# Product order, staging of the last row tiles and VectorE order in a Strassen-Winograd matmul with logsumexp

## The chip, the cores and the metric

The kernel runs on one core of one Trainium2 chip. The metric is the device time of one execution in microseconds. Each kernel is run several times, together with the kernel before on the same chip. Most executions of a kernel agree within 0.3%; some of the kernel before are up to 2.5% slower and are left out as slow runs. Ratios in this document are the mean time of one kernel's fast runs over that of the other's, so they are not quite the ratio of the medians that are quoted. A profiled execution's span is about 2 us shorter than its time. All spans and positions are of profiled runs.

Engines in the profile: PE is the matmul side of TensorE, PEld its weight loads, DVE is VectorE, ACT is ScalarE, POOL is GpSimd, SP is SyncE.

## The reference

```python
m, k, n = 1024, 4096, 4096
a = np.random.randn(m, k).astype(np.float32)
b = np.random.randn(k, n).astype(np.float32)
x = np.matmul(a, b)
return special.logsumexp(x, axis=-1).astype(np.float32)
```

## The kernel before

Both operands become fp16. The columns of B are taken in eight blocks of 512. The rows of A are eight tiles of 128, taken in pairs; a pair, a block and all of k make a *quad*. A quad is computed by the Strassen-Winograd scheme: seven products M1 to M7 of 16 matmuls (128x128 weights, 256 columns) in place of eight. Two PSUM rows, r0 and r1, hold the four quarters of the result: c11 and c12 are the halves of r0, c21 and c22 those of r1. ScalarE copies some products out of PSUM, VectorE adds them, then come a row maximum on VectorE and an exponential on ScalarE. VectorE also makes the sums of B that some products need (T1, T4, T6 in new tiles, T3 and T7 in place) and the sums of A; the rows of one pair in `aT` are a *slab* of A (one text below also calls a quarter of a B block so). The last quad of a step (step 6 apart), in which most sums of the next block are made, is called a *tail*. In the code, KP is 16 (all of k, 256 rows at a time), GI is 4 (a quarter of k), H is 256 columns, MT is 8 row tiles and MP 4 row pairs.

The work has this shape in time. Block 0 is multiplied plainly while A and B arrive (until about 63 us). Step 0 is block 1 for three row pairs at once (the *joint* quads). Steps 1 to 6 are blocks 2 to 7, four quads each. Two more quads finish blocks 0 and 1 for the last row pair. That pair is not transposed on TensorE as the first three are: GpSimd's DMA queue casts the two row tiles to fp16 in DRAM (the *staging* copies), and SyncE's DMA queue transposes them from there into `aT`. Step 1's fourth quad needs them first, after VectorE has made five sums of that slab.

```python
a_m = a.rearrange("(p mt) k -> mt p k", mt=MT)       # row tile, 128 rows, k
...
        def load(self, lo, hi):                       # a quarter of a B block
            nc.gpsimd.dma_start(out=self.raw[lo // GI][...], in_=b_rows[:, lo:hi, :, ts(self.nb, FD)])
...
        if more:
            ...
                nxt = plan[step + 1][0]().load_all()
        if step == 0:
            a16 = dram_pool.tile([2, P, K], f16, name="a16")
            for m in range(2):
                nc.gpsimd.dma_start(out=a16[m], in_=a_m[MT - 2 + m])      # staging
            for m in range(2):
                nc.sync.dma_start_transpose(
                    aT[:, :, :, MP - 1, m, :].rearrange("p i t c -> p (i t) c"), a16[m])
...
            s = fix_pool.tile([P, 4, H], f32, name=f"s_{step}_{q}", tag="s")   # one buffer
            x, e = s[:, 1::2], s[:, 0:2]              # x[:, 0] is the place of e[:, 1]
            ...                                       # M1, M5 -> r0; copy e; M2, M6 -> r1
            nc.scalar.copy(out=s[:, 2], in_=c21)
            flush()                                   # exponentials of the quad before
            add(s[:, 2], s[:, 2], e[:, 1])
            sub(s[:, 0], s[:, 2], e[:, 0])
            ...
            m3(c12)
            nc.scalar.copy(out=x[:, 0], in_=c12)
            m7(c11)
            m4(c21)
            nc.scalar.copy(out=x[:, 1], in_=c21)
            sub(x, x, s[:, 0::2])
            add(c22, c22, x[:, 0])
            add(c11, c11, x[:, 1])
            ...
            for h in range(2):
                lse_max(rows[h], 2 * q + h, nb)
                pending.append(...)                   # lse_exp, run by the next flush
            if step == 1 and q == 1:
                a_sums_early(slice(0, KP), MP - 1)    # sums of the last slab of A
                a_sums_late(slice(0, KP), MP - 1)
```

## Time and profile before

| | before |
|---|---|
| time, median of 20 runs | 455.34 us (453.89 to 462.8) |
| span of the profiled run | 453.5 us |
| PE busy | 93% |
| one product of 16 matmuls, start to start | 1.747 us |
| a full quad, start to start | 12.85 us (7 x 1.747 = 12.23) |
| nine last products of the three joint quads | 83.95 to 113.0 us |

These are lines of the page of the kernel before. Each digit is the busy share of one of 40 slices of 11.3 us in tenths; `PEclk` is the granted TensorE clock, `DMA` the busy share of the 16 DMA engines, `GB/s` what they moved.

```profile
span 453.5 us, 8512 instructions
PE 422.7 (93%) x3647; PEld 350.5 (77%) x3647; DVE 258.7 (57%) x566; ACT 109.6 (24%) x278; POOL 73.1 (16%) x114
...
PEclk9999999986999999999999999999999999999998
DMA  8999999999994069300990059400990049599000
```

TensorE is nearly always busy; DMA is full for the first 12 slices, then works about 40% of the time (the mean of the other 28 digits). PE dips in the slices around 90 to 113 us, and there the clock falls too. The waits of PE say why (columns: who waited, for whom; us in total, times, longest):

```profile
PE acc_2_0_761 L366 <- ACT s_2_1130 L493: 4.5, 1, 4.5
PE acc_1_0_759 L366 <- ACT s_1_1061 L493: 3.3, 1, 3.3
...
PE acc_2_0_1471 L366 <- ACT s_2_1473 L493: 1.1, 1, 1.1
...
PE acc_0_0_2295 L366 <- ACT s_0_2297 L493: 0.5, 1, 0.5
```

L493 is ScalarE's copy of M3's result, and the waiter is M7. The last line is one of 25 alike, one for nearly every quad. The timeline shows one of these quads (start, duration, engine, line, instruction, how many):

```profile
211.71 0.60 PE L366 MATMUL acc_3_0_2139<-b_3_1205,aT 128*128 128x256 f16 x4
...
212.35 0.37 ACT L493 COPY s_3_2141<-acc_3_0_2139 128x256 f32<-128x256 f32 x1
...
212.77 0.60 PE L366 MATMUL acc_3_0_2139<-b_0_1202,aT 128*128 128x256 f16 x4 [0.46 <-ACT s_3_2141 L493]
```

M3's last four matmuls start at 211.71 us and M7 would follow 0.44 us later, at 212.15. It starts at 212.77: 0.62 us are lost per quad. The two products write the halves of one row, and the copy reads that row.

The last row tiles cost nothing visible here. Their two staging copies are down 34 us after they are issued, most of it spent in the queue, and the transposes run beside the loads of the next B block. These are the lines of the DMA issues (out, in, queue, count, size of one, us from issue to landing):

```profile
a_752<-in_a_dram POOLq DMA_DIRECT2D x2, 1024.0 KB, 34.0
...
aT<-a_752 SPq DMA_TRANSPOSE x2, 20.7
```

### The profile page before, as it was taken

The numbers are of one execution on the slowest core, as the hardware profiler recorded it, in microseconds if no ns is written. First come the engines' busy times: TensorE is split into PE (matmuls) and PEld (weight loads), VectorE is DVE, ScalarE is ACT, GpSimd is POOL, SyncE is SP. The second block draws the span as 40 slices with busy tenths as digits, with TensorE's granted clock in tenths as the row PEclk, the third lists the DMA queues.
The fourth block names the chain that finished last, engine by engine and source line by source line (L and its number), as shares of the span: only waits on it lengthen the run. The fifth ranks groups of instructions, "written<-read, shape, count | busy, mean of one in ns | idle before, by whom it ended". The sixth has DMA issues, their size and how long they took to land.

```text
span 453.5 us, 8512 instructions
## 1 busy us (share of the span) xinstructions
PE 422.7 (93%) x3647; PEld 350.5 (77%) x3647; DVE 258.7 (57%) x566; ACT 109.6 (24%) x278; POOL 73.1 (16%) x114
## 2 busy tenths in 40 slices
PE   7999999976999999999999999999999999999994
PEld 2554568854888888888888888888888888888883
DVE  1557687555737595218832585127922485175995
ACT  1222240122222122222221222222211222222214
POOL 7776751003000030001100030000200030110000
PEclk9999999986999999999999999999999999999998
DMA  8999999999994069300990059400990049599000
GB/s 120 202 203 203 194 202 206 207 214 219 197 180 71 1 103 207 63 1 2 198 172 1 1 90 207 76 2 1 187 185 1 1 77 207 89 192 180 1 2 0
DMA packets 57493, 52.97 MB, mean 117 GB/s; under 512 B 10096, under 2 KB 57200, under 8 KB 57200
## 3 DMA queue, kind: packets, MB, share of 16 engines
q0 software_dynamic: 49056, 50.34, 67.4%
q1 hardware_dynamic: 8400, 2.10, 3.1%
q8 instruction: 28, 0.46, 0.4%
q14 instruction: 9, 0.07, 0.0%
HBM read 100.66 MB, written 2.10 MB: 227 GB/s over the span
## 4 chain that ended last, share of the span: by engine, by line
PE 79%; DVE 9%; ACT 6%; DMA 4%; issue 1%; POOL 1%; DVEq 0%; ACTq 0%; POOLq 0%
DMA tb<-in_a_dram 4%; PE acc_0_0_757 L366 2%; PE acc_3_0_4311 L366 2%; PE acc_1_0_4043 L366 2%; PE acc_2_0_3631 L366 2%; PE acc_1_0_2423 L366 2%; PE acc_3_0_2139 L366 2%; PE acc_2_0_2011 L366 2%; PE acc_1_0_2963 L366 2%; PE acc_3_0_2679 L366 2%; PE acc_2_0_2551 L366 2%; PE acc_1_0_1883 L366 2%; PE acc_3_0_1599 L366 2%; PE acc_2_0_4175 L366 2%; PE acc_3_0_3759 L366 2%; PE acc_1_0_3503 L366 2%
## 5 line engine op out<-in xcount | busy, mean ns | idle before, releaser
L366 PEld LDWEIGHTS <-aT 128*128 128x128 f16 x1856 | 183.8, 99 | 48.2 <-issue 25.3
L366 PEld LDWEIGHTS <-s_71 128*128 128x128 f16 x464 | 45.4, 98 | 5.5
L366 PEld LDWEIGHTS <-s_73 128*128 128x128 f16 x464 | 45.4, 98 | 5.3
L366 PEld LDWEIGHTS <-s_72 128*128 128x128 f16 x464 | 45.4, 98 | 5.3
L192 POOL DMA_DIRECT2D tb<-in_a_dram x48 | 26.0, 544 | 7.5 <-PE tps_98 L203 1.5
L203 PEld LDWEIGHTS <-tb 128*128 128x128 f16 x192 | 13.9, 99 | 16.7 <-DMA tb<-in_a_dram 10.3
L221 PEld LDWEIGHTS <-aT 128*128 128x128 f16 x192 | 16.8, 98 | 11.9 <-ACT aT L216 0.3
L216 ACT COPY aT<-tps_98 128x512 f16<-128x512 f16 x24 | 14.0, 585 | 44.3 <-PE tps_98 L203 44.3
L214 DVE COPY aT<-tps_97 128x512 f16<-128x512 f16 x24 | 10.2, 425 | 25.5 <-PE tps_97 L203 25.4
L84 DVE TENSOR_TENSOR aT<-aT 128x256 f16<-128x256 f16 (+2 forms) x54 | 16.0, 350 | 0.0
L203 PE MATMUL tps_97<-ident,tb 128*128 128x128 f16 x96 | 9.6, 224 | 1.7 <-DMA tb<-in_a_dram 1.7
L203 PE MATMUL tps_98<-ident,tb 128*128 128x128 f16 x96 | 9.3, 219 | 1.0 <-DMA tb<-in_a_dram 1.0
L81 DVE TENSOR_TENSOR s_71<-aT 128x256 f16<-128x256 f16 (+1 forms) x25 | 8.1, 323 | 2.1 <-ACT aT L216 2.1
L138 POOL DMA_DIRECT2D b_0_1747<-in_b_dram x1 | 0.9, 881 | 50.8 <-PE acc_3_0_1599 L366 50.8
L138 POOL DMA_DIRECT2D b_0_2827<-in_b_dram x1 | 0.9, 890 | 47.9 <-PE acc_3_0_2679 L366 47.9
L138 POOL DMA_DIRECT2D b_0_2287<-in_b_dram x1 | 0.9, 878 | 47.9 <-PE acc_3_0_2139 L366 47.9
L138 POOL DMA_DIRECT2D b_0_3907<-in_b_dram x1 | 0.9, 881 | 47.9 <-PE acc_3_0_3759 L366 47.9
L138 POOL DMA_DIRECT2D b_0_3367<-in_b_dram x1 | 0.9, 878 | 47.9 <-PE acc_3_0_3219 L366 47.9
L81 DVE TENSOR_TENSOR s_73<-aT 128x256 f16<-128x256 f16 (+1 forms) x25 | 8.1, 324 | 0.0
L81 DVE TENSOR_TENSOR s_72<-aT 128x256 f16<-128x256 f16 (+1 forms) x25 | 8.1, 323 | 0.0
L282 PE MATMUL acc_1_96<-s_73 128*128 128x512 f16 x15 | 6.5, 570 | 1.2 <-DVE s_73 L285 1.2
L138 POOL DMA_DIRECT2D aT<-in_b_dram x4 | 3.5, 890 | 24.2 <-PE acc_1_1_4044 L366 24.2
(1045 smaller groups left out, 899.0 us busy)
## 6 DMA issues: line engine op xcount, KB each, us to landing
tb<-in_a_dram POOLq DMA_DIRECT2D x48, 128.0 KB, 5.9
aT<-in_b_dram POOLq DMA_DIRECT2D x4, 1024.0 KB, 14.7
a_752<-in_a_dram POOLq DMA_DIRECT2D x2, 1024.0 KB, 34.0
b_0_83<-in_b_dram POOLq DMA_DIRECT2D x4, 256.0 KB, 6.0
b_1_84<-in_b_dram POOLq DMA_DIRECT2D x4, 256.0 KB, 6.2
b_2_85<-in_b_dram POOLq DMA_DIRECT2D x4, 256.0 KB, 6.4
b_3_86<-in_b_dram POOLq DMA_DIRECT2D x4, 256.0 KB, 6.2
b_0_87<-in_b_dram POOLq DMA_DIRECT2D x2, 512.0 KB, 8.6
```

The costliest lines, as they stand in the source:

```text
L81: nc.vector.tensor_tensor(out=o, in0=x, in1=y, op=ALU.add)
L84: nc.vector.tensor_tensor(out=o, in0=x, in1=y, op=ALU.subtract)
L138: nc.gpsimd.dma_start(out=self.raw[lo // GI][:, lo % GI : lo % GI + hi - lo], in_=b_rows[:, lo:hi, :, ts(self.nb, FD)],)
L192: nc.gpsimd.dma_start(out=slot, in_=a_m[m, :, k0 * P : (k0 + kn) * P])
L203: nc.tensor.matmul(pst[:, ts(j, P)], src[:, ts(j, P)], ident, is_transpose=True, start=(j == 0), stop=(j == kn - 1),)
L214: nc.vector.tensor_copy(out=dst, in_=v)
L216: nc.scalar.copy(out=dst, in_=v)
L221: nc.tensor.matmul(pt, aT[:, i, kp, m // 2, m % 2, :], blk0.raw[i // GI][:, i % GI, kp, :], start=(done[m] == 0), stop=(done[m] == KT - 1),)
L282: nc.tensor.matmul(acc[2][1], zeros[:, 0:P], zeros[:, 0:FD], start=True, stop=True)
L366: nc.tensor.matmul(c, lhs(i), rhs(i), start=(start and i == 0), stop=(i == KP - 1), skip_group_check=True,)
```

## The change

The change has three parts. The product order in each quad becomes M3, M4, M7, so that M4, which writes the other row, runs while ScalarE copies M3's result. The last two row tiles come in k halves: a staging copy for both tiles and one half of k, then two half transposes, and so on; the slab's sums are split to match, and GpSimd holds back the last two of the four B loads of step 2 (block 3) until the first half is transposed, by an instruction that reads one of its rows (the *gate*). In the joint quads VectorE makes the sums of one quarter of the next B block per quad, and the rest afterwards.

```diff
+                if step == 1:
+                    nxt.load(0, GI)
+                    nxt.load(GI, 2 * GI)
+                    nc.gpsimd.tensor_copy(
+                        out=ident[0:1, 0:2], in_=aT[0:1, 0, 0, MP - 1, :, 0]
+                    )
+                    nxt.load(2 * GI, 3 * GI)
+                    nxt.load(3 * GI, KP)
...
-            a16 = dram_pool.tile([2, P, K], f16, name="a16")
-            for m in range(2):
-                nc.gpsimd.dma_start(out=a16[m], in_=a_m[MT - 2 + m])
...
+            KH = K // 2
+            for h in range(2):
+                a16 = dram_pool.tile([2, P, KH], f16, name=f"a16_{h}")
+                nc.gpsimd.dma_start(out=a16, in_=a_m[MT - 2 :, :, ts(h, KH)])
+                for m in range(2):
+                    nc.sync.dma_start_transpose(
+                        aT[:, ts(h, KP // 2), :, MP - 1, m, :].rearrange(...), a16[m])
...
-                for g in {0: [0], 1: [1], 2: [3]}[q]:
-                    for what in ("t1", "t6", "t3"):
-                        nxt.make(what, g * GI, (g + 1) * GI)
+                for what in ("t1", "t6"):
+                    nxt.make(what, q * GI, (q + 1) * GI)
...
+            if step == 1 and q == 2:
+                a_sums_early(slice(KP // 2, KP), MP - 1)
+                a_sums_late(slice(KP // 2, KP), MP - 1)
             m3(c12)
             nc.scalar.copy(out=x[:, 0], in_=c12)
-            m7(c11)
             m4(c21)
             nc.scalar.copy(out=x[:, 1], in_=c21)
+            m7(c11)
             sub(x, x, s[:, 0::2])
             add(c22, c22, x[:, 0])
+            if not tail:
+                lse_max(r1, 2 * q + 1, nb)
             add(c11, c11, x[:, 1])
-            if joint and q == 1:
-                for what in ("t1", "t6", "t3"):
-                    nxt.make(what, 2 * GI, 3 * GI)
+            if joint and tail:
+                for what in ("t1", "t6"):
+                    nxt.make(what, 3 * GI, KP)
+                nxt.make("t3")
...                                         # the maximum of r0 comes last
             if step == 1 and q == 1:
-                a_sums_early(slice(0, KP), MP - 1)
-                a_sums_late(slice(0, KP), MP - 1)
+                a_sums_early(slice(0, KP // 2), MP - 1)
+                a_sums_late(slice(0, KP // 2), MP - 1)
```

More of the change, by code (lines that the diff above doesn't have):

```diff
@@ L344 @@
             else:
-                nxt = plan[step + 1][0]().load_all()
-        if step == 0:
-            a16 = dram_pool.tile([2, P, K], f16, name="a16")
-            for m in range(2):
-                nc.gpsimd.dma_start(out=a16[m], in_=a_m[MT - 2 + m])
-            for m in range(2):
-                nc.sync.dma_start_transpose(
-                    aT[:, :, :, MP - 1, m, :].rearrange("p i t c -> p (i t) c"), a16[m]
-                )
+                nxt = plan[step + 1][0]()
+                if step == 1:
[6 more added lines that the diff above has]
+                    nxt.load(3 * GI, KP)
+                else:
+                    nxt.load_all()
+        if step == 0:
+            KH = K // 2
[4 more added lines that the diff above has]
+                    nc.sync.dma_start_transpose(
+                        aT[:, ts(h, KP // 2), :, MP - 1, m, :].rearrange("p i t c -> p (i t) c"),
+                        a16[m],
+                    )
         quads = {}
@@ L491 @@
                 nxt.make("t4")
+            if step == 1 and q == 2:
+                a_sums_early(slice(KP // 2, KP), MP - 1)
+                a_sums_late(slice(KP // 2, KP), MP - 1)
             m3(c12)
             nc.scalar.copy(out=x[:, 0], in_=c12)
-            m7(c11)
             m4(c21)
             nc.scalar.copy(out=x[:, 1], in_=c21)
+            m7(c11)
             sub(x, x, s[:, 0::2])
             add(c22, c22, x[:, 0])
+            if not tail:
+                lse_max(r1, 2 * q + 1, nb)
             add(c11, c11, x[:, 1])
-            rows = (r0, r1)
-            if joint and q == 1:
-                for what in ("t1", "t6", "t3"):
-                    nxt.make(what, 2 * GI, 3 * GI)
+            if joint and tail:
+                for what in ("t1", "t6"):
+                    nxt.make(what, 3 * GI, KP)
+                nxt.make("t3")
             if tail:
@@ L507 @@
                 nxt.make("t7")
-            for h in range(2):
-                lse_max(rows[h], 2 * q + h, nb)
-                pending.append(lambda h=h, q=q, nb=nb, rows=rows: lse_exp(rows[h], 2 * q + h, nb))
+            if tail:
+                lse_max(r1, 2 * q + 1, nb)
+            lse_max(r0, 2 * q, nb)
+            for r, m in ((r1, 2 * q + 1), (r0, 2 * q)):
+                pending.append(lambda r=r, m=m, nb=nb: lse_exp(r, m, nb))
             if step == 1 and q == 1:
-                a_sums_early(slice(0, KP), MP - 1)
-                a_sums_late(slice(0, KP), MP - 1)
+                a_sums_early(slice(0, KP // 2), MP - 1)
+                a_sums_late(slice(0, KP // 2), MP - 1)
             if early and q == 1:
```

## The prediction

> **What bounds the kernel now.** TensorE. In the profile page PE is busy 93% of the 453.5 us span. The timeline shows:
>
> - Until about 84 us DMA feeds it (windows: 200 to 207 GB/s). The change does not touch this.
> - The three joint quads' last nine products, 83.95 to 113.0 us: a product takes 1.747 us, so 15.7 of these 29.05 us are work. The waits of PE name the copy of M3's result by ScalarE (line 493), 3.3 and 4.5 us; then the granted clock falls to 0.72 (window 95:113).
> - Then 26 quads. A full one takes 12.845 us against 7 x 1.747 = 12.23 us: M7 waits for that copy, listed as 0.46 us, 0.615 us start to start. One waits 1.1 us, behind the slab-3 sums (5.8 us of VectorE from 141.9 us).
>
> In the chain of waits everything from 422.4 us to the end is VectorE or ScalarE.
>
> **Why M7 waits.** M3 and M7 write the two halves of one accumulator row. The Trainium skill, "PSUM — Partial Sum Buffer", section "PSUM bank collisions raise a hardware error", says two engines may not use one bank and quadrant at once, so the read of c12 and writes of c11 are ordered. The trace agrees: M7 starts 0.43 us after the copy starts. M4 writes the other row; between M3 and M7 it covers the copy (0.37 us).
>
> **Steady quads.** The 19 quads of steps 2 to 6 before the last of step 6 save 0.615 us each: 11.7 us. After a tail quad, VectorE finishes the maxima 8.5 us into the next quad, then come two exponentials and the copy (1.1 us to the release); M7 starts at 10.5 us: no stall.
>
> **Joint quads.** VectorE makes fewer tiles there. Laying out the engines with measured durations gives a 0.65 us stall in quad 1 and the end near 100.3 us instead of 113.0. Price: 4 more VectorE makes after the last joint quad, so its maxima end near 110.6 us and M7 of step 1's first quad stalls about 1.1 us. Step 1 ends near 150.4 us instead of 165.0: 14.6 us saved.
>
> **Last row tiles.** The packets show the transpose queue at 279 GB/s alone but 40 GB/s beside B loads at 155 GB/s: 256 B and 1024 B packets one to one, as "DMA: Bandwidth & Descriptors", section "Queues, rings and completion order", says of its round robin. B loads now come earlier (99 us), so without the gate the transposes would land near 141 us. With it: first two B loads done about 123 us, first half transposed 124.5, second 128.5, held loads by 140. The half sums need them at 127.8 and 134 us.
>
> **End.** VectorE is full from 8 us into step 6's last quad, so the two last quads' savings buy nothing (0 to 0.2 us).
>
> **Sum.** 14.6 + 11.7 = 26.3 us. Predicted time 429.0 us, span near 427. Range 426.5 to 434. Chances: faster 0.97, same 0.02, slower 0.01.
>
> **What would show it.** Right: no listed PE wait on the M3 copy in steps 2 to 6, quads of 12.23 us; step 1 starting at 100 to 101 us; clock near 1 in 84 to 113 us; the chain still VectorE for the last 27 us. Wrong: transposes after 135 us and VectorE idle on DMA before the second half sums; M7 of step 1's first quad stalling over 2 us; waits in quads after tails.
>
> **What would make it wrong.** Transposes starved, stalling quad 3 of step 1 by 2 to 5 us; B of step 2 landing late; ScalarE's queue holding copies longer than laid out.

## The result

The changed kernel takes 453.44 us (median of 10 runs, 452.51 to 454.55) against 455.34 us. The ratio is 0.9956, with a 95% interval of 0.9934 to 0.9977: the same within 2%, where 429.0 us and a gain of 5.8% (1 - 429.0/455.34) had been predicted.

These lines of the changed kernel's page answer to those shown of before. `PE` and `PEclk` have a hole at 136 to 158 us, and in front of it DMA, full before, is at 2 tenths.

```profile
span 451.9 us, 8525 instructions
PE 416.2 (92%) x3647; PEld 350.2 (77%) x3647; DVE 260.5 (58%) x571; ACT 108.8 (24%) x278; POOL 74.8 (17%) x115
...
PE   6999999999991099999999999999999999999993
...
PEclk9899999999997589999999999999999999999998
DMA  8999999999229996940199009900594019899000
```

All the waits of PE of the changed kernel that concern the quads:

```profile
PE acc_2_0_1475 L378 <- ACT s_2_1477 L507: 21.6, 1, 21.6
...
PE acc_0_0_1764 L378 <- ACT s_0_1766 L507: 0.9, 1, 0.9
PE acc_0_0_1214 L378 <- ACT s_0_1216 L507: 0.8, 1, 0.8
```

The half microsecond of every quad is gone, as are the 3.3 and 4.5 us of the joint quads. In their place stands one wait of 21.6 us, in step 1's third quad. M1 of selected quads starts at these times:

| M1 starts at (us) | before | changed | rows leading (an experiment below) |
|---|---|---|---|
| step 1, first quad | 112.84 | 100.67 | 99.03 |
| step 1, third quad | 138.53 | 126.09 | 124.44 |
| step 1, fourth quad | 152.03 | 161.62 | 136.67 |
| step 2, first quad | 164.87 | 173.84 | 148.90 |
| step 6, fourth quad | 408.96 | 407.22 | 381.20 |

So 12.4 us were won by the third quad of step 1 (138.53 - 126.09), 22 us were lost within one quad, and the other quads' gains then brought the kernel back to 1.7 us ahead. The timeline shows what the third quad waited for:

```profile
127.27 0.69 DVE L87 TENSOR_REDUCE negmax<-acc_1_0_1342 128x1 f32<-128x512 f32 x1
...
134.82 1.91 PE L378 MATMUL acc_2_1_1476<-tb,aT 128*128 128x256 f16 x16
136.48 15.10 SPq L362 DMA_TRANSPOSE aT<-a_0_752  x2
...
154.34 0.69 DVE L81 TENSOR_TENSOR s_71<-aT 128x1024 f16<-128x1024 f16 x1 [26.37 <-DMA aT<-a_0_752]
...
157.86 0.37 ACT L507 COPY s_2_1477<-acc_2_0_1475 128x256 f32<-128x256 f32 x1 [22.87 <-DVE s_2_1477 L81]
...
158.28 1.01 PE L378 MATMUL acc_2_0_1475<-b_0_744,aT 128*128 128x256 f16 x4 [21.55 <-ACT s_2_1477 L507]
```

Read it from the bottom. M7 waits for the copy of M3's result. The copy writes `x[:, 0]`, the place of `e[:, 1]`, and so waits until VectorE's add has read that. The add stands in VectorE's queue behind the first half of the slab's sums, and these wait from 128 us for the transposes, which land after 154 us. SyncE issues the first transposes only at 136.48 us; in the kernel before it was 104.50 us. They wait for the staging copies:

```profile
a_0_752<-in_a_dram POOLq DMA_DIRECT2D x1, 1024.0 KB, 65.5
a_1_756<-in_a_dram POOLq DMA_DIRECT2D x1, 1024.0 KB, 65.1
```

The copies take 65 us to land instead of 34, though they carry as many bytes as before. GpSimd's own rows hardly show it: the issue of one takes 1.09 us, where it took 0.55 us before. The Trainium skill says so in "Perfetto Trace Analysis", section "Per-instruction lifecycle: what the profiler-reported window actually captures": the data movement of a DMA lies outside the window of the instruction that issues it. The chain of waits does not name the culprit either. In a window from 100 to 165 us it begins with

```profile
0.68 135.78 another core or an unknown queue
```

because it does not follow a DMA issued so long before its landing. What is left is the throughput by stretches (us; busy time and count of instructions of each engine; the last three numbers are the clock, DMA's share and GB/s; the records of packets overlap, so the share reads 1.24 where DMA is full):

```profile
84.00:95.00 11.00, 10.90 (x101) 9.62 (x100) 7.40 (x15) 3.73 (x11) 0.00 (x0) 1.00 1.24 207
95.00:113.00 18.00, 17.20 (x159) 15.27 (x157) 16.42 (x30) 5.30 (x15) 1.82 (x2) 1.00 1.06 165
113.00:126.00 13.00, 13.00 (x122) 11.66 (x120) 4.02 (x9) 3.05 (x8) 0.00 (x0) 1.00 0.27 55
126.00:139.00 13.00, 10.73 (x99) 9.47 (x97) 1.90 (x4) 2.31 (x6) 0.00 (x0) 1.00 0.50 61
139.00:152.00 13.00, 0.00 (x0) 0.00 (x0) 0.00 (x0) 0.00 (x0) 0.00 (x0) 0.58 1.19 84
```

From 113 to 126 us the copies are nearly alone on the engines and move 55 GB/s at a DMA share of 0.27, close to 4 of 16 engines (0.25). The kernel before had 197 GB/s in the same stretch.

### The profile page after: what moved, and what is told of

It reads as the page before. It is cut to its first block, busy times and chain, and to the rows that moved or that the text cites. A ratio compares the mean times of both kernels' runs of the same rounds, so it can differ in the third digit from the quotient of the medians.

```text
span 451.9 us, 8525 instructions
## 1 busy us (share of the span) xinstructions
PE 416.2 (92%) x3647; PEld 350.2 (77%) x3647; DVE 260.5 (58%) x571; ACT 108.8 (24%) x278; POOL 74.8 (17%) x115
## 4 chain that ended last, share of the span: by engine, by line
PE 51%; another core or an unknown queue 30%; DVE 10%; DMA 7%; ACT 1%; issue 1%; SPq 0%; POOL 0%; POOLq 0%; DVEq 0%; ACTq 0%
DMA aT<-a_0_752 4%; DMA b_3_1208<-in_b_dram 3%; DVE tb L81 2%; PE acc_2_0_4184 L378 2%; PE acc_0_0_3384 L378 2%; PE acc_2_0_3100 L378 2%; PE acc_3_0_2688 L378 2%; PE acc_0_0_3924 L378 2%; PE acc_3_0_3768 L378 2%; PE acc_1_0_2432 L378 2%; PE acc_0_0_2304 L378 2%; PE acc_2_0_2020 L378 2%; PE acc_1_0_1892 L378 2%; PE acc_2_0_3640 L378 2%; PE acc_1_0_3512 L378 2%
## 5 line engine op out<-in xcount | busy, mean ns | idle before, releaser
L203 PEld LDWEIGHTS <-tb 128*128 128x128 f16 x192 | 14.9, 99 | 15.7 <-DMA tb<-in_a_dram 4.2
L81 DVE TENSOR_TENSOR s_71<-aT 128x256 f16<-128x256 f16 (+1 forms) x26 | 8.2, 317 | 31.7 <-DMA aT<-a_0_752 26.4
L378 PE MATMUL acc_2_0_1475<-b_0_744,aT 128*128 128x256 f16 x8 | 1.6, 340 | 21.6 <-ACT s_2_1477 L507 21.6
L84 DVE TENSOR_TENSOR aT<-aT 128x256 f16<-128x256 f16 (+1 forms) x56 | 16.2, 343 | 0.0
```

Of the source, the lines that this page charges most:

```text
L81: nc.vector.tensor_tensor(out=o, in0=x, in1=y, op=ALU.add)
L84: nc.vector.tensor_tensor(out=o, in0=x, in1=y, op=ALU.subtract)
L203: nc.tensor.matmul(pst[:, ts(j, P)], src[:, ts(j, P)], ident, is_transpose=True, start=(j == 0), stop=(j == kn - 1),)
L378: nc.tensor.matmul(c, lhs(i), rhs(i), start=(start and i == 0), stop=(i == KP - 1), skip_group_check=True,)
```

## The experiments

**The theory and its rivals.** The kernel before copies each row tile by itself; the leading dimension of such a copy is its 128 rows. The changed kernel copies both tiles at once, and the leading dimension is the 2 tiles. The Trainium skill, "DMA: Bandwidth & Descriptors", section "Why a DMA increments its semaphore by 16 and not by 1", under "How many engines (k)", says that the number of engines is the largest one up to 16 that divides the slowest dimension (of size over 1) of both sides: here 2. Two copies of 2 engines make 4 engines. This is theory S. Its rivals blame the halves (pieces of 4 KB instead of 8 KB, four small transposes), the gate, or the new order itself.

The packet records of the trace decide much of it. The following table is counted from them (start, duration, size and queue of each packet); it is no view of the page. "Engines" is the summed duration of the staging packets over the stretch from the first to the last.

| | staging packets (us) | one packet | engines | half of the transposed packets / all moved (us) | 4-byte packets on GpSimd's queue |
|---|---|---|---|---|---|
| before | 97.4 to 109.0 | 8192 B, 625 ns | 13.75 | 112.6 / 140.6 | 1696 |
| changed | 96.7 to 138.2 | 4096 B, 324 ns | 4.00 | 153.0 / 157.8 | 5280 |
| rows leading | 96.1 to 107.9 | 4096 B, 324 ns | 14.06 | 123.4 / 129.7 | 1696 |
| one copy per tile and half | 96.6 to 108.4 | 4096 B, 324 ns | 14.08 | 123.8 / 130.2 | 1728 |
| the same, leading 2 | 96.7 to 121.7 | 2048 B, 174 ns | 7.14 | 138.8 / 143.7 | 8896 |
| no gate | 96.8 to 108.3 | 4096 B, 324 ns | 14.41 | 135.2 / 140.5 | 1696 |
| order only | 97.3 to 109.5 | 8192 B, 627 ns | 13.11 | 136.2 / 141.1 | 1696 |
| no halves | 96.3 to 108.5 | 8192 B, 626 ns | 13.21 | 123.8 / 128.9 | 1696 |
| before, with this staging | 97.1 to 138.5 | 4096 B, 324 ns | 4.01 | 164.7 / 169.3 | 5280 |

The changed kernel's 41.5 us are 128 packets of 324 ns one after the other: each copy has 256 packets, on two engines. With all engines the same packets take the same 324 ns each, so neither the size of the pieces nor the DRAM makes a packet slower. All results below were correct against the reference.

**Rows leading.** One thing is altered in the changed kernel:

```diff
-                nc.gpsimd.dma_start(out=a16, in_=a_m[MT - 2 :, :, ts(h, KH)])
+                nc.gpsimd.dma_start(
+                    out=a16.rearrange("m p k -> p m k"),
+                    in_=a_m[MT - 2 :, :, ts(h, KH)].rearrange("m p k -> p m k"),
+                )
```

> The changed kernel with one thing altered: each of the two staging copies of the last row tiles names the 128 rows as its leading dimension (128 x 2 x 2048) instead of the two row tiles (2 x 128 x 2048). Same number of copies, same bytes, same contiguous pieces. Theory S (spray): the copy with a leading dimension of 2 ran on 2 of the 16 engines, so both together on 4, at 52 to 56 GB/s from 97 to 138 us; with 128 leading it uses all 16, both copies are down by about 109 us, the transposes by about 129 us, the 21.6 us wait of M7 in step 1's third quad is gone, and the time is 427 to 431 us. Rival H (halves): copies of 4 KB rows (instead of 8 KB) into DRAM are slow in themselves, or four small transposes are; then staging stays near 54 GB/s and the time stays at 450 to 454 us. Rival G (gate): the wait on the first half's transposes is what holds all; then the time stays above 445 us.

Measured: 428.14 us (4 runs, 427.75 to 429.3), ratio 0.9415 (0.9384 to 0.9445). The kernel before scattered from 454.41 to 466.03 us in this job, and the verdict is unclear, as it is for all four kernels of this job (this one and the next three), though each one's slowest run is over 13 us below the fastest run of the kernel before. The same kernel repeated later gave 428.28 us and 0.940 (0.9367 to 0.9433). The only wait on the copy of M3 that remains is the one of step 1's first quad, and the same stretches now read:

```profile
PE acc L381 <- ACT s L510: 0.8, 1, 0.8
```

```profile
113.00:126.00 13.00, 13.00 (x122) 11.65 (x120) 4.09 (x9) 3.05 (x8) 0.35 (x2) 1.00 1.18 181
126.00:139.00 13.00, 13.00 (x122) 11.65 (x120) 10.09 (x19) 3.05 (x8) 1.58 (x2) 1.00 1.21 198
139.00:152.00 13.00, 13.00 (x122) 11.65 (x120) 9.94 (x19) 3.05 (x8) 3.50 (x4) 1.00 0.29 43
```

DMA moves 181 and 198 GB/s where it moved 55 and 61, and PE is busy throughout. Halves, gate and order are all still in this kernel, so none of the three rivals holds the 25 us. The difference of the two spans (451.9 - 425.9 = 26.0 us) is accounted for: 1.6 us stood between the two runs before step 1 began, and all of it already at 83 to 85 us, before any staging packet moved (the last nine products of the joint quads start at 84.69 and 83.04 us; in the kernel before and five other runs of these experiments at 83.08 to 83.95), so it is not the copies' doing, and I count it as scatter of the loading stage; 23.3 us come between there and M1 of step 1's fourth quad (the wait of M7, and M7 itself, which took 3.3 instead of 1.75 us at a clock of 0.63 from 152 to 165 us); 1.1 us come in step 2, where the held B loads were late.

**One copy per tile and half.** The same four half tiles in four copies.

```diff
-                nc.gpsimd.dma_start(out=a16, in_=a_m[MT - 2 :, :, ts(h, KH)])
+                for m in range(2):
+                    nc.gpsimd.dma_start(out=a16[m], in_=a_m[MT - 2 + m, :, ts(h, KH)])
```

> The changed kernel with each staging copy split in two, one per row tile and half (four copies of 128 x 2048). Theory S expects the same as with the rows leading: 16 engines, copies down by about 109 us, 427 to 431 us. A rival that blames the number of bytes per copy or the 4 KB pieces expects no gain, 450 to 454 us.

Measured: 428.20 us (428.00 to 428.78), ratio 0.9409 (0.9390 to 0.9429); staging used 14.08 engines. It does as well as rows leading, so it is not the number of copies.

**The same four copies with a leading dimension of 2.** This asks whether the leading 2 does it, or only the two tiles in one copy, and whether the cost goes with the number of engines.

```diff
-                    nc.gpsimd.dma_start(out=a16[m], in_=a_m[MT - 2 + m, :, ts(h, KH)])
+                    nc.gpsimd.dma_start(
+                        out=a16[m].rearrange("p (c j) -> c p j", c=2),
+                        in_=a_m[MT - 2 + m, :, ts(h, KH)].rearrange("p (c j) -> c p j", c=2),
+                    )
```

> Four staging copies, one per row tile and half, as in the version with one copy per row tile, but each written with a leading dimension of 2 (two column blocks: 2 x 128 x 1024). Theory S: each copy gets 2 engines, the four together 8, so the 2.1 MB take about half as long as the 41 us they took on 4 engines: about 20 us, down near 118 us at roughly 100 GB/s; then the transposes end near 137 us, M7 of step 1's third quad waits 1 to 3 us instead of 21.6, and the time is 429 to 435 us. A rival that says it was two row tiles in one copy (not the leading 2) expects 427 to 431 us and staging down at 109 us.

Measured: 439.61 us (438.23 to 441.24), ratio 0.9659. Four copies of 2 engines gave 7.14 engines and 25.0 us of staging, against 4.00 and 41.5 us of the changed kernel and about 14 and 12 us with the rows leading. Staging ended at 121.7 us, a little later than theory S put it, and the time lies above its range: M7 waited 8.5 us, not 1 to 3. The transposes were the part that I sized too small. From 125 to 132 us the packets show 76 to 78 GB/s of B, half of the rate it has on all engines beside transposes, so I take it that the rest of the first two B loads sat on the eight engines that had been busy with staging. The transposes moved at about 40 GB/s for as long as that lasted, though the other eight engines should have been free.

**No gate.** Rows leading, and

```diff
-                if step == 1:
-                    nxt.load(0, GI)
-                    ...
-                else:
-                    nxt.load_all()
+                nxt.load_all()
```

> Rows leading in the staging copies, and the gate taken out (the four B loads of step 2 issued at once). What the prediction said of the gate: without it the transposes share packets one to one with B loads (40 GB/s beside 155) and land near 140 us; the first half sums would wait until about 135 us, M7 of step 1's third quad about 3 us, time 2 to 4 us above the gated version, 430 to 434 us. If the gate is worthless the time equals the gated version's; if the gate itself costs (B late), it is lower.

Measured: 435.22 us (434.66 to 436.51), ratio 0.9566. The transposes end at 140.5 us, as the prediction said of a kernel without the gate. The gate is worth 7.1 us here (435.22 - 428.14), twice what I had expected, since the first half sums started at 136.9 us and not at 135, M7 waited 5.4 us, and the clock fell in that wait (0.74 from 139 to 152 us). The wait is VectorE's, on the transposes:

```profile
136.87 1.90 DVE L81 TENSOR_TENSOR s<-aT 128x1024 f16<-128x1024 f16 x3 [10.17 <-DMA aT<-a]
```

**Order only.** The changed kernel with staging and transposes as before, no gate, and the sums of the slab in one piece.

```diff
-            KH = K // 2
-            for h in range(2): ...             # staging and transposes by halves, and the gate
+            a16 = dram_pool.tile([2, P, K], f16, name="a16")
+            ...                                # as in the kernel before
-            if step == 1 and q == 2: ...       # second half of the sums
-                a_sums_early(slice(0, KP // 2), MP - 1)
+                a_sums_early(slice(0, KP), MP - 1)
```

> The changed kernel without its staging part: product order M3, M4, M7 and the moved VectorE work, but whole-row staging and whole transposes as before, no gate, slab-3 sums in one piece. B loads come 8 us earlier than before and share packets with the transposes, which end near 141 us; then 5.8 us of sums stand in front of the third quad's adds, so M7 there waits about 11 us. Expected 437 to 443 us. A reading in which the product order alone gives all 26 us expects 427 to 431 us.

Measured: 442.19 us (441.45 to 442.90), ratio 0.9714 (0.9698 to 0.9731), faster by 2.9%. M7 waited 11.4 us. The new order brings the B loads forward and the transposes do not follow, so the middle part of the change is needed; as it was written it cost more than leaving it out (453.44 us).

**No halves.** Gate and half sums stay, staging and transposes are by whole rows as before.

```diff
-            KH = K // 2
-            for h in range(2): ...             # staging and transposes by halves
+            a16 = dram_pool.tile([2, P, K], f16, name="a16")
+            ...                                # as in the kernel before
```

> The changed kernel with the gate and the sums in halves, but staging and transposes by whole rows as before (two copies of 128 x 4096, two transposes); the gate then waits for both. From the rows-leading run: first B loads done 121 us, all 2.1 MB transposed by about 130 us, held loads landed by about 144 us. The first half sums wait 2 us that the third quad does not feel (its adds wait for ScalarE until 133 us anyway). Expected 427 to 431 us, that is, cutting the transposes in k halves is worth under 2 us once the gate is there. If the halves matter, 432 to 437 us.

Measured: 429.05 us (428.50 to 429.47), ratio 0.9428 (0.9412 to 0.9444). Beside a gate the halves of the transfers are worth about 1 us or less, which these runs do not resolve: the intervals of this ratio and of the rows-leading one overlap, and the two ran on different chips. Nearly the whole gain of the middle part could have been had with the gate and the split sums, which leave the copies as they were.

**The kernel before with this staging.** Only the lines of staging and transposes are put into the kernel before; its order and sums stay and there is no gate.

```diff
-            a16 = dram_pool.tile([2, P, K], f16, name="a16")
-            ...                                # two copies, two transposes
+            KH = K // 2
+            for h in range(2): ...             # as in the changed kernel
```

> The kernel before with only the changed kernel's staging and transposes put in (two copies of 2 x 128 x 2048, four half transposes; old product order, no gate, sums in one piece). Theory S, whatever the product order: staging takes 41 us (97 to 138 us) on 4 engines; the four B loads of step 2 leave a quarter of their bytes on those 4 engines, which drain at about 41 GB/s beside the transposes until about 163 us; transposes end near 168 us; the slab-3 sums, queued at 142 us, hold VectorE, and M7 of step 1's third quad waits some 25 to 28 us. Time 476 to 490 us. If the slow staging is an effect of the new order or the gate, the time stays within 455 to 460 us.

Measured: 486.02 us (484.19 to 487.41), ratio 1.0675 (1.0647 to 1.0703), slower. Staging took 41.4 us on 4.01 engines again, so it owes nothing to the new order. The longest wait of M7 was 31.3 us. I take it that the gate, which lets only two B loads queue up behind the copies, had spared the changed kernel part of this; order and sums differ too, and no run separates them.

**The old sums in the joint quads.** Rows leading, with the third part undone.

```diff
-                for what in ("t1", "t6"):
-                    nxt.make(what, q * GI, (q + 1) * GI)
+                for g in {0: [0], 1: [1], 2: [3]}[q]:
+                    for what in ("t1", "t6", "t3"):
+                        nxt.make(what, g * GI, (g + 1) * GI)
...
-            if joint and tail: ...
+            if joint and q == 1:
+                for what in ("t1", "t6", "t3"):
+                    nxt.make(what, 2 * GI, 3 * GI)
```

> Rows leading in the staging copies, with the third named part undone: in the joint quads VectorE makes T1, T6 and T3 as the kernel before did (one slab in quads 0 and 2, two in quad 1). VectorE then does 1.8 us more inside quad 1 before the maxima; laid out with measured durations, M7 of the third joint quad waits about 2 us for the copy of M3 (it stands behind two exponentials that wait for the maxima), and the 0.8 us wait in step 1's first quad goes. Net 1 to 2 us slower than rows leading in the same job. If that part is what removes the joint quads' waits, 6 us or more slower; if it is worth nothing, equal within 0.5 us.

> The rows-leading version again, only as the partner of the run with the old VectorE order on the same chip. Expected 428 us, within 1 us of its first run.

Measured: 428.80 us (428.74 to 428.97) with the old sums, 428.28 us (427.74 to 428.93) without. The ratios, 0.9412 and 0.9400, have overlapping intervals. The longest wait on the copy of M3 is 1.2 us with the old sums and 0.8 us with the new. This part is worth about 0.5 us, which the ratios do not resolve, and less than I had laid out. The 12 us that the joint quads won come, then, from what is left: the product order, with the row maxima that were moved along with it. No run undoes the maxima alone.

**A faster version.** Rows leading, and three moves on VectorE: the maxima of the last joint quad before its T4 and T7, T3 and T4 for the last-but-one quad made a quad earlier, half of T6 of the last quad made before the adds.

```diff
-            if early and q == MP - 1:
+            if early and q == MP - 2:
                 nxt.make("t3")
                 nxt.make("t4")
...
+            if joint and tail:
+                lse_max(r1, 2 * q + 1, nb)
+                lse_max(r0, 2 * q, nb)
             if tail:
                 nxt.make("t4")
```

> Rows leading in the staging copies, and VectorE work moved: the maxima of the last joint quad before T4 and T7 (removes 0.8 us of wait in step 1's first quad), T3 and T4 of the last-but-one step made one quad earlier, half of T6 of the last step made before the adds. The last two quads then become TensorE's again: VectorE's chain ends about 3 us earlier. Expected 423 to 427 us. If the end is not bound by VectorE, 427 to 429 us.

Measured: 425.71 us (425.03 to 425.86), ratio 0.9350 (0.9336 to 0.9364): faster than both kernels and about 2.4 us below rows leading (428.14, another job). The wait in step 1's first quad fell from 0.8 to 0.4 us. The end is shorter (42.6 us from M1 of step 6's last quad at 381.44 us, against 44.7), but it did not become TensorE's as I had expected: in the chain of waits nearly everything from 394.8 us on is still VectorE or ScalarE. Which of the three moves brought how much was not tested.

## Why the prediction was wrong

- **What bounds the kernel, and why M7 waits.** Right. With M4 between M3 and M7 no quad of steps 2 to 6 waits for the copy, but for one late B load in the changed kernel (0.9 us). The rule of the Trainium skill's "PSUM — Partial Sum Buffer", section "PSUM bank collisions raise a hardware error", on two engines and one bank was the right guide: the waits were only where M7 wrote the row that the copy read.
- **Steady quads.** Right. 12.23 us, to the hundredth, where 12.85 stood.
- **Joint quads.** Right in the number, and in the mechanism as far as the product order goes. Step 1 began at 100.67 us (predicted 100.3), clock 1.00 from 84 to 113 us. The wait in joint quad 1 was 0.3 us (93.69 against 91.67 + 1.75) instead of 0.65, and that of step 1's first quad was listed as 0.8 instead of 1.1 us. The parts of VectorE's work were over-rated: undoing them costs about 0.5 us.
- **Last row tiles. This step failed.** The prediction put it so: "With it: first two B loads done about 123 us, first half transposed 124.5, second 128.5, held loads by 140." It costed the transposes and the loads packet by packet, and has no term for the staging copies in front of them, so it took for granted that they would run as before; they carried the same bytes. They took 41.5 us (96.7 to 138.2) instead of 11.6. The cause, shown by three layouts of the same bytes, is the leading dimension of 2 in the copy: 4.00 engines busy instead of 14. All that followed, transposes at 154 us, VectorE idle for 26.4 us, M7 waiting 21.6 us, comes from it. The page that tells how many engines a copy gets had the answer; the prediction read it for its round robin only.
- **With that one term mended the rest holds.** Rows leading ran in 428.14 us (predicted 429.0), with half of the transposed packets moved by 123.4 us, all by 129.7 us (predicted 124.5 and 128.5). Stage by stage it fits too, so this is no luck of opposite errors: step 1 began at 99.03 and ended at 148.90 us (predicted 100.3 and 150.4), and 0.9 us of that lead stood already at the start of the last nine products (83.04 against 83.95 us). The sentence that transposes without the gate would land near 141 us came out at 140.5.
- **End.** Right. From M1 of step 6's last quad to the end the kernel before took 44.6 us (453.53 - 408.96) and the changed one 44.7 us (451.9 - 407.22), though its two quads were 0.6 us shorter each.
- **The signs of failure** that the prediction named did show: transposes after 135 us and VectorE idle on DMA, only in front of the first half of the sums already. Its range, 426.5 to 434 us, and its chance of 0.02 for "same" were too sure: they allowed 2 to 5 us for starved transposes and nothing for a slow copy.

The size of the gain that went missing is known, then. By the rows-leading run it is about 25 us of time (453.44 - 428.14), and one rewritten access pattern brings it back.

## What to carry to other kernels

When copies are merged or cut differently, look at the leading dimension of the new access pattern and not only at bytes and packet sizes: two copies led by the 2 tiles kept 4 DMA engines busy, where copies led by 128 rows kept about 14 busy. A DMA that became slow is found in the throughput of a stretch in which little else moves and in the time to landing, not in the instruction that issues it. A change that brings consumers forward also brings their loads forward, so each transfer that used to hide behind them needs its own costing, and queues that share packets one to one may need a gate.

## What the Trainium skill lacked or had wrong

- "DMA: Bandwidth & Descriptors", "How many engines (k)": it agrees with these runs (leading 2: 4.00 engines for two copies, 7.14 for four; leading 128: 13.1 to 14.4). Beyond a bandwidth per engine of about 27 GiB/s (its table "Specifications") it does not say what such a copy yields: 52 to 56 GB/s written for two casting DRAM to DRAM copies on 2 engines each, at 324 ns for a packet of 4096 B and 625 ns for one of 8192 B. Counted on the fp32 side, which is twice as long, 324 ns are 25 GB/s per engine, near the page's figure; counted on the fp16 side they are half of that.
- The same page, "Why a DMA increments its semaphore by 16 and not by 1", has all 16 engines post one increment for a GpSimd-queue copy; two copies more did add 32 packets of 4 bytes (1728 against 1696). It does not mention the many more that a copy on few engines has: 5280 instead of 1696, that is 3584 more, or 14 x 128 for each of two copies; 8896 instead of 1728, again 14 x 128 for each of four. That they belong to the 14 unused engines is an inference from that count.
- The same page, "Queues, rings and completion order", gives packets of typically 9 to 17 descriptors as the unit of the round robin. In the packet records here the transpose queue and the B loads take turns record by record: 385 of 256 B against 381 of 1024 B in the 2.5 us from 110 us of the rows-leading run, in an order of which 97% repeats after 32 records, 16 of each: one of each for every engine. Whether such a record is a descriptor or a packet of one the trace does not say.
- No page says that a DMA transpose goes at the pace of its most loaded engines: with B's leftovers on 4 engines (changed kernel, 140 to 150 us) the transposes moved 35 to 42 GB/s, as with B on all 16 (40 GB/s), and over 200 GB/s once those were gone. That the transposes keep the engines in step is my reading; no run tested it by itself.
- The same page, "Latency and other measured facts", gives 261 GB/s as the effective rate of a DMA transpose with a non-contiguous middle dimension and about 350 to 400 for a contiguous one. In the 2.5 us from 110 us of the kernel before it moved 279 GB/s; later, alone, 212 and 252 GB/s (changed kernel, from 152.5 and 155 us). These lie around the lower figure; which of the two cases the transposes here are was not settled.
